# A convolution in 64x64 instead of 32x32 matmul tiles, and all V projections ahead of the spatial mixing

## The chip, the cores and the metric

The kernel runs on all eight cores of one Trainium2 chip (two dies of four cores), one sequence per core. The metric is the device time of the slowest core, in microseconds (us). Most executions agree within 0.3%. Some fall in a second, slower state, in which one die has a lower clock (the kernel before at 2910.64 us: one die's cores at 0.91 to 0.92, the other's at 0.98 to 0.99). The **granted clock** is the TensorE clock that the trace records as allowed, 1.00 being full speed.

Engine names: PE is TensorE (matmuls), PEld its weight loads, ACT is ScalarE, DVE is VectorE, POOL is GpSimd, SP is SyncE, which issues transfers.

## The reference, cut to what matters

One inference step of a decoder trunk with four layers. The part of a layer that matters here:

```python
h = rmsnorm(x, norm1);  z = h @ w_in
# group B: spatial gating inside chunks of 128 rows
b_out = zu * (einsum('hts,bnshc->bnthc', tril(sgu_w), zv) + sgu_b)
# group C: GLU, then a causal depthwise convolution of 31 taps over 384 channels
c_in  = zc[..., :D_C] * sigmoid(zc[..., D_C:])
c_out = silu(layernorm(causal_dwconv(c_in, state, conv_w, conv_b)))
x = x + concat([a_out, b_out, c_out]) @ w_out
x = x + conv_ffn(rmsnorm(x, norm2))
```

Each core has 2048 prompt rows and 64 sample rows. The sample rows need a convolution state that is brought in separately.

## The kernel before

A depthwise convolution has no sum over channels, so on PE it is a banded matrix per channel. The kernel puts 16 channels times 8 time phases on the 128 partitions (a "group"; there are 24). Five shifted matmuls (`k`) cover the 31 taps, and each weight matrix is block diagonal in the channel. Because it is block diagonal it can be cut into small tiles: 4 channels x 8 phases is a 32x32 tile. Two groups (a "pair") are worked on together, `h = 0, 1`. The second one goes to other column strips of the array than the first, so eight of the sixteen 32x32 tiles are in use.

```python
TW = 32
for q in range(12):                                   # twelve pairs
    pb2 = [bank(), bank()]                            # two PSUM banks
    for k in range(NK):                               # 5 shifts
        fin_k = k == NK - 1
        for part in range(1 if fin_k else 2):         # 256 prompt columns, then 16 of the sample state
            for i in range(4):
                for h in range(2):
                    g = 2 * q + h
                    pi = slice(32 * i, 32 * i + 32)
                    po = slice(32 * (i ^ h), 32 * (i ^ h) + 32)
                    src = QS[pi, g, 16*k:16*k+16] if part else Q[j][pi, g % 8, k:k + (MW if fin_k else MB)]
                    dst = pb[po, MB:MW] if part else pb[po, 0:MW if fin_k else MB]
                    matmul(dst, bands.v[j][pi, g % 8, k, :], src, start=(k == 0 and not part), stop=fin_k)
    if q >= 4 and q % 2 == 0: stats(q - 4, q - 2)     # LayerNorm sums, 128x128 matmuls of 272 columns
    # ACT: y[first half] = psum + bias          DVE: y[second half] = psum + bias
    # ACT: sq = square(y)                       POOL: ym = sum of the halves
    # DVE: yq = sum of the halves of sq (of the pair before)
    # [layer 0 only: one step of the pooling of the last tile, on DVE]
```

That is 72 matmuls per pair, each with its own weight load: 144 PE instructions, 1728 per layer. After the convolution the V projections (8 matmuls of 384 columns each), the LayerNorm on DVE, the swishes on ACT and the spatial mixing overlap. V16, V0, V1 come before the convolution, V2 and V3 right after it, then:

```python
for c in range(4, 13):
    vproj(c)
    ...                                   # DVE normalises, ACT applies swish, in between
jobs = [("s", 0), ("v", 13), ("s", 1), ("v", 14), ("v", 15), ("s", 2), ("s", 4), ("s", 3)]
for kind, a in jobs:                      # "s": mixing and gating of tile a, "v": V projection a
    ...
```

The convolution result goes through HBM (a "hop") to return to channel-major order. POOL copies it into place, and the output projection reads it.

Of the kernel before, what the change touches and what calls it, by code (L numbers as in the profile page):

```python
# [11 lines left out]
DEPTH = 4  # L12
# [28 lines left out]
NG = 24  # L41
NK = 5
# [5 lines left out]
SLOT = 2048  # L48
RING = 6 * SLOT
NVB = 17  # L50
TW = 32

class Res:
    __slots__ = ("name", "w", "r", "excl")
# [173 lines left out]
def build_nc():  # L228
# [18 lines left out]
    bnd = din("bnd", [DEPTH, 128, NG * NK * TW])  # L247
# [21 lines left out]
    with ExitStack() as st:  # L269
        S = Sched(nc, st)  # L270
# [22 lines left out]
        AR = Arena(ARENA_T, AW)  # L293
# [31 lines left out]
        DBD = [S.dsem(f"dbd{t}") for t in range(8)]  # L325
# [20 lines left out]
        W = Ring(S, WSA, RING, plan)  # L346

        order = [4, 0, 1, 2, 3]
        order0 = [0, 4, 1, 2, 3]
# [167 lines left out]
        class Bands:  # L517
            def __init__(self, l):
                self.l = l
                self.v, self.R = [], []  # L520
                for b in range(3):
                    v, r = AR.carve(f"dg{b}_", 12768 + 640 * b, 640, 1)
                    self.v.append(v.bitcast(BF16).rearrange("p (g k n) -> p g k n", g=8, k=NK))
                    self.R += r

            def load(self, t):
                S.dma("pool", self.v[t].rearrange("p g k n -> p (g k n)"), bnd[self.l][:, 1280 * t:1280 * (t + 1)], DBD[t], writes=[self.R[t]])

        nrm = Norm(NB, VT_N1)
        nrm.small = AR.carve("sqs", NB, 256, 8)[1]  # L530
# [39 lines left out]
        for l in range(DEPTH):  # L570
            sz_v, Rsz, sc_v, Rsc = stp
            cin, Rcin, Rcs = [], [], []
            for j, a in enumerate((0, 4 * MW, 5308)):
                v, r = AR.carve(f"cin{j}", a, 4 * MW, 2)
# [9 lines left out]
            for j in range(3):  # L584
                S.op("pool", lambda e: e.tensor_copy(cin[j][:, 0:4, MB:MW], sc_v[:, 64 * j:64 * j + 64].rearrange("p (f m) -> p f m", f=4)),
                     reads=[Rsc], writes=[Rcs[j]])
# [278 lines left out]
            vb, Rvb = [None] * NVB, [None] * NVB  # L865

            def vslot_new(c):
                v, r = AR.carve(f"vb{c}_", 14688 + 192 * ((c + 1) % NVB) if c == 16 or c < 13 else 8640 + 192 * (c - 13), 192, 1)
                vb[c], Rvb[c] = v.bitcast(BF16), r[0]

            for i in (16, *range(13)):
                vslot_new(i)
            vs_v, Rvs = AR.carve("vstg", 17376, 384, 1)
            w_v = [W.get(4) for _ in range(2)]
# [1 line left out]
            def vproj(c):  # L876
                rows = 128 if c < 16 else 64
                ti = c // 4
                pb, Rpb = bank()
                for k in range(KC):  # L880
                    S.op("pe", lambda e: e.matmul(pb[0:rows, 0:384], H[:, k, c * 128:c * 128 + rows], w_v[k // 4][1][:, k % 4, :], start=(k == 0), stop=(k == 7)),  # L881
                         reads=[w_v[k // 4][2], RH[k][ti]], writes=[Rpb], inc=(k == 7))
                S.op("act", lambda e: e.copy(vb[c][0:rows], pb[0:rows, 0:384]), reads=[Rpb], writes=[Rvb[c]])  # L883
                if c == 16:
                    S.op("dve", lambda e: e.tensor_copy(vs_v[0:64, 0:384], pb[0:64, 0:384]), reads=[Rpb], writes=[Rvs[0]])
                    out_dma(o_v[l], vs_v[0:64, 0:384], [Rvs[0]], "vstg")
# [6 lines left out]
            for q in range(12):  # L893
                pb2 = [bank(), bank()]
                j = q // 4
                if q % 4 == 0:
                    r0, r1 = [AR.carve(f"y{j}{h}", 2176 * j + 1088 * h, 1088, 4)[1] for h in range(2)]
                    yj.append((ARENA_T[:, 2176 * j:2176 * (j + 1)], r0 + r1))
                rr = [Rq[j][0], Rq[j][1], Rqs, bands.R[j]]
                for k in range(NK):  # L900
                    fin_k = k == NK - 1
                    for part in range(1 if fin_k else 2):
                        for i in range(4):
                            for h in range(2):
                                g = 2 * q + h
                                pi, po = slice(32 * i, 32 * i + 32), slice(32 * (i ^ h), 32 * (i ^ h) + 32)
                                pb, Rpb = pb2[h]
                                src = QS[pi, g, 16 * k:16 * k + 16] if part else Q[j][pi, g % 8, k:k + (MW if fin_k else MB)]
                                dst = pb[po, MB:MW] if part else pb[po, 0:MW if fin_k else MB]
                                S.op("pe", lambda e: e.matmul(dst, bands.v[j][pi, g % 8, k, :], src, start=(k == 0 and not part), stop=fin_k, skip_group_check=True),  # L910
                                     reads=rr, writes=[Rpb], inc=(fin_k and i == 3))
                if q >= 4 and q % 2 == 0:
                    stats(q - 4, q - 2)
                y_v, Ry = yj[j]
                ql = q % 4
                y = y_v[:, ql * 2 * MW:(ql + 1) * 2 * MW]
                cbs = [CVQ[:, 2 * q + h:2 * q + h + 1] for h in range(2)]
                ph = [p_[0][:, 0:MW] for p_ in pb2]
                R0, R1 = pb2[0][1], pb2[1][1]
                Ryq = Ry[2 * ql:2 * ql + 2]  # L920
                sq_v, Rsq_ = sqt[q % 2]
                (ym, Rym), (yq, Ryq2) = sums[2 * (q % 4)], sums[2 * (q % 4) + 1]
                S.op("act", lambda e: e.activation(y[:, 0:MW], ph[0], AF.Identity, bias=cbs[0]), reads=[R0, Rcvq], writes=Ryq[0:1])
                S.op("dve", lambda e: e.tensor_scalar(y[:, MW:2 * MW], ph[1], cbs[1], None, ALU.add), reads=[R1, Rcvq], writes=Ryq[1:2])
                S.op("act", lambda e: e.activation(sq_v, y, AF.Square), reads=Ryq, writes=Rsq_)
                S.op("pool", lambda e: e.tensor_tensor(ym, y[:, 0:MW], y[:, MW:2 * MW], ALU.add), reads=Ryq, writes=Rym)
                while psq:
                    psq.pop(0)()
                psq.append(lambda sq_v=sq_v, Rsq_=Rsq_, yq=yq, Ryq2=Ryq2: S.op("dve", lambda e: e.tensor_tensor(yq, sq_v[:, 0:MW], sq_v[:, MW:2 * MW], ALU.add), reads=Rsq_, writes=Ryq2))
                if steps:  # L930
                    next(steps.pop(0), None)
                if q == 8 and l == 0:
                    assert not steps
                    prep(0)
                    S.dma("sp", FB[:, 0:576], bb_d[0], DM["bb"], writes=[Rfb])
# [1 line left out]
            W.fill()  # L937
            w_u = [W.get(4) for _ in range(2)]
            stats(8, 10)
            for i in (13, 14, 15):  # L940
                vslot_new(i)
            for c in (2, 3):
                vproj(c)
# [109 lines left out]
            def quad():  # L1053
                if quads:
                    j, h = quads.pop(0)
                    ln_quad(j, h)
                    silus.extend((j, h, a) for a in range(4))

            def act_side(n=1):
                for _ in range(n):  # L1060
                    if silus:
                        silu(*silus.pop(0))

            for c in range(4, 13):
                vproj(c)
                if c >= 5:
                    act_side(1)
                if c in (4, 6, 8, 10, 11, 12):
                    quad()
            mixes = [(j, ti) for ti in order0 for j in range(2)]  # L1070
            jobs = [("s", 0), ("v", 13), ("s", 1), ("v", 14), ("v", 15), ("s", 2), ("s", 4), ("s", 3)]
            for kind, a in jobs:
                if kind == "v":
                    vproj(a)
                    if a == 15:
                        for w in w_v:
                            W.done(w[0])
                else:
                    mixed = mixv(a)
                    ts = [addb(a, b, *mixed[b]) for b in range(2)]  # L1080
                    for b in range(3):
                        if b == 1:
                            ts.append(addb(a, 2, *mixed[2]))
                        sgu(a, b, *ts[b])
                        act_side(3 if a == 0 else 2)
                        if mixes and not silus:
                            pmix(*mixes.pop(0))
                    if a in (1, 2, 3):
                        reo[a - 1]()
            while mixes:  # L1090
                pmix(*mixes.pop(0))
            for w in w_u:
# [247 lines left out]

def _conv_rows():
    g, c = np.arange(D_C) // 16, np.arange(D_C) % 16
    return 16 * g + (c ^ (4 * (g % 2)))

def _cat_cols(parts):
    return np.ascontiguousarray(np.concatenate([p.reshape(DEPTH, 128, -1) for p in parts], axis=2))
# [39 lines left out]
    return dict(wt=wt, wts=ws.reshape(DEPTH, 64, 256), bb=np.ascontiguousarray(bb).reshape(DEPTH, 128, 3 * 192))  # L1386

def _phase_layouts(conv_w, conv_b, cnorm_g, cnorm_b):
    bd = np.zeros((DEPTH, 16, 8, NG, NK, 4, 8), np.float32)
    c = np.arange(16)  # L1390
    wg = conv_w.reshape(DEPTH, 31, NG, 16)
    for k in range(NK):
        for fi in range(8):
            for fo in range(8):
                i = 8 * k - 2 + fi - fo
                if 0 <= i < 31:
                    bd[:, c, fi, :, k, c % 4, fo] = wg[:, i].transpose(2, 0, 1)
    vq = np.stack([conv_b, cnorm_g, cnorm_b], axis=1)[:, :, _conv_rows()].reshape(DEPTH * 3 * NG, 16)
    return bd.reshape(DEPTH, 128, NG * NK * TW), np.ascontiguousarray(np.repeat(vq.T, 8, axis=0))

# [69 lines left out]
```

## Time and profile before

| | before |
|---|---|
| kernel time, fast runs | 2731.26 to 2733.41 us |
| PE busy | 97% of the span |
| first convolution matmul to V4, four layers, mean of the cores | 29.5, 31.8, 30.1, 31.1 us |
| V4 to output projection | 45.2, 45.2, 44.7, 44.7 us |

"First convolution matmul to V4" is called **the stage** below. It is read off the trace, core by core, and holds the convolution, V2, V3 and the statistics.

The page of the profile of before (slowest core): its span, PE's share, and PE's busy tenths and granted clock in 40 slices.

```profile
span 2726.5 us, 55276 instructions; the slowest of 8 cores (2716.4 to 2726.5 us)
...
PE 2643.4 (97%) x18494; PEld 1283.8 (47%) x18762; DVE 1724.1 (63%) x2955; ACT 1424.6 (52%) x2705; POOL 600.9 (22%) x840
...
PE   8899999999989999999998999999999899999998
...
PEclk9899999999989999999998999999999999999999
```

The kernel is bound by PE almost everywhere. The few slices below 9 are the places to look at. The windows view of before over the four stages has span, busy time of each engine, granted clock, and DMA share and GB/s:

```profile
93.70:123.90 30.20, 22.09 (x906) 15.00 (x906) 16.36 (x34) 14.60 (x27) 13.72 (x16) 0.72 0.14 36
766.20:799.40 33.20, 23.70 (x905) 15.73 (x905) 8.66 (x24) 14.46 (x26) 11.23 (x16) 0.69 0.20 41
1435.90:1466.40 30.50, 23.44 (x905) 15.35 (x905) 8.78 (x24) 14.54 (x27) 10.69 (x15) 0.72 0.10 26
2102.80:2132.10 29.30, 21.44 (x906) 14.64 (x906) 8.77 (x24) 14.36 (x27) 11.23 (x16) 0.83 0.12 29
```

No engine is near full in any of them (PE 21 to 24 of about 30 us, the others less), and the granted clock is about 0.7. So what is PE waiting for? The timeline of PE in layer 1 (start, length, what; in brackets the idle time before and what ended it; L910 is the convolution, L864 the statistics):

```profile
766.25 1.75 PE L910 MATMUL ps<-arena 32*32 32x256 bf16 x133
768.88 1.77 PE L910 MATMUL ps<-arena 32*32 32x16 bf16 x126 [0.88 <-issue]
773.32 2.05 PE L910 MATMUL ps<-arena 32*32 32x16 bf16 x101 [2.67 <-issue]
...
777.59 2.33 PE L910 MATMUL ps<-arena 32*32 32x256 bf16 x126 [0.63 <-issue]
781.25 1.06 PE L864 MATMUL ps<-arena,oneb 128*128 128x272 bf16 x4 [1.34 <-issue]
```

Two things are to be seen. 126 matmuls take 1.77 us, so PE is fast while it runs. And every gap is ended by "issue": no semaphore and no engine was waited for. The transfer view of before lists the instruction queue; first the 28.5 us of layer 1's convolution, then 28.5 us inside the feed-forward part:

```profile
q8 instruction: 7, 0.11, 1.6%
...
q8 instruction: 1, 0.02, 0.2%
```

The trace records these packets one by one. Here is when each of layer 1 landed (start plus its duration), and when PE issued again after the gap that followed:

```
16,384-byte packet landed at   767.51  771.99  776.25  779.69  784.00  788.28  792.88
PE issues again at             768.88  773.32  777.59  781.25  785.33  789.58  794.31
difference, us                   1.37    1.33    1.34    1.56    1.33    1.30    1.43
```

Every one of the seven packets is followed by a restart of PE 1.3 to 1.6 us later. How many instructions a packet brings can be counted. On all eight cores, the gaps over 0.2 us in layer 1's convolution stand before the same matmuls, the 134th, 260th, 383rd, 509th, 633rd and 758th (statistics counted). They are 123 to 126 matmuls apart, so 246 to 252 instructions with the weight loads. With the semaphore instructions that the trace records for PE there are 255 to 257 instructions from one restart to the next. The whole run agrees: core 1, of which no record is missing, has 40,173 PE instructions and 157 packets, 255.9 per packet.

There are two smaller waits further on: PE waits for DVE in the first mixing tiles (L1026), and in layers 0 and 3 for the reorder copies at the output projection (L1115). The timeline of PE before:

```profile
819.35 0.41 PE L1014 MATMUL ps<-wt_s,arena 128*32 128x128 bf16 x16 [0.35 <-DVE arena L1026]
...
174.29 8.02 PE L1115 MATMUL ps<-arena,wsall 128*128 128x512 bf16 x28 [3.78 <-POOL arena L997]
```

### The profile page before, as it was taken

What the parts mean: (1) busy time and instruction counts of PE and PEld (TensorE: products, weight loads), DVE (VectorE), ACT (ScalarE), POOL (GpSimd) and SP (SyncE); (2) the same over time, 40 slices, a digit from 0 to 9 for tenths busy, and PEclk for the clock granted to TensorE, in tenths of its full rate; (3) what the DMA queues carried; (4) which work ended last, traced back from release to release, by engine and by line L of the source; (5) the groups of instructions that cost most, each with busy time, mean ns of one, the idle gap of its engine ahead of it and who ended that gap; (6) DMA issues with size and microseconds to landing.
All of it is one profiled execution on the core that took longest, in us unless ns stands there. A gap on an engine that the chain in (4) does not pass through costs nothing.

```text
span 2726.5 us, 55276 instructions; the slowest of 8 cores (2716.4 to 2726.5 us)
## 1 busy us (share of the span) xinstructions
PE 2643.4 (97%) x18494; PEld 1283.8 (47%) x18762; DVE 1724.1 (63%) x2955; ACT 1424.6 (52%) x2705; POOL 600.9 (22%) x840
## 2 busy tenths in 40 slices
PE   8899999999989999999998999999999899999998
PEld 3544444444444444444445444444444444444444
DVE  5658656566856765656685675565677567565566
ACT  5446627176354653627535473554753547264575
POOL 4544000003315300000412610000060260000005
PEclk9899999999989999999998999999999999999999
DMA  9342222223233322222223232222223413222213
GB/s 239 87 97 50 37 39 36 39 40 61 50 73 88 56 38 38 37 39 40 53 67 84 60 63 38 38 38 39 40 48 84 108 26 57 40 37 38 40 30 128
DMA packets 82181, 159.56 MB, mean 59 GB/s; under 512 B 10928, under 2 KB 43952, under 8 KB 81840
## 3 DMA queue, kind: packets, MB, share of 16 engines
q0 software_dynamic: 29840, 96.65, 20.9%
q1 hardware_dynamic: 52064, 59.35, 7.1%
q8 instruction: 157, 2.57, 0.4%
q14 instruction: 120, 0.98, 0.1%
HBM read 226.78 MB, written 28.39 MB: 94 GB/s over the span
## 4 chain that ended last, share of the span: by engine, by line
PE 91%; issue 3%; DMA 2%; DVE 2%; ACT 2%; SPq 1%; POOL 0%; DVEq 0%; ACTq 0%; POOLq 0%
PE ps L1205 23%; PE ps L1199 23%; PE ps L1115 16%; PE ps L1277 15%; PE ps L595 7%; PE ps L1037 2%; PE ps L910 2%; PE ps L881 1%; DMA hop<-arena 1%; PE ps L864 1%; DMA X<-win 1%; SPq L139 1%; DMA arena<-hop 0%; DVE H L449 0%; ACT arena L883 0%
## 5 line engine op out<-in xcount | busy, mean ns | idle before, releaser
L1205 PE MATMUL ps<-H,wsall 128*128 128x512 bf16 (+1 forms) x3500 | 697.3, 342 | 1.0
L1199 PE MATMUL ps<-H,wsall 128*128 128x512 bf16 (+1 forms) x3404 | 687.7, 341 | 6.1
L1219 DVE SCALAR_TENSOR_TENSOR arena<-arena,vt_s 128x512 f32<-128x512 f32 (+1 forms) x440 | 289.6, 658 | 384.0 <-ACT arena L1218 367.3
L1214 ACT COPY arena<-ps 128x512 f32<-128x512 f32 (+1 forms) x440 | 223.7, 509 | 575.4 <-PE ps L1199 527.1
L1115 PE MATMUL ps<-arena,wsall 128*128 128x512 bf16 (+2 forms) x2581 | 464.6, 339 | 9.8 <-POOL arena L997 7.3
L1205 PEld LDWEIGHTS ps<-H,wsall 128*128 128x128 bf16 x3520 | 301.8, 98 | 332.6
L1199 PEld LDWEIGHTS ps<-H,wsall 128*128 128x128 bf16 x3520 | 301.8, 98 | 332.6
L1277 PE MATMUL ps<-arena,wsall 128*128 128x512 bf16 (+1 forms) x2200 | 399.1, 342 | 2.1
L1218 ACT ACTIVATE arena<-ps,vt_s 128x512 f32<-128x512 f32 (+1 forms) x440 | 309.0, 702 | 66.0 <-ACT arena L1214 2.8
L1115 PEld LDWEIGHTS ps<-arena,wsall 128*128 128x128 bf16 x2624 | 220.9, 98 | 245.3 <-issue 12.6
L420 POOL TENSOR_TENSOR arena<-arena 128x512 f32<-128x512 f32 (+2 forms) x273 | 293.7, 1076 | 149.2 <-ACT arena L414 119.6
L1221 DVE SCALAR_TENSOR_TENSOR arena<-arena,vt_s 128x512 f32<-128x512 f32 (+1 forms) x440 | 289.5, 658 | 47.0 <-DVE arena L1219 1.4
L1280 DVE TENSOR_TENSOR X<-ps,X 128x512 f32<-128x512 f32 (+1 forms) x320 | 184.5, 595 | 196.5 <-PE ps L1277 196.4
L414 ACT ACTIVATE arena<-X 128x512 f32<-128x512 f32 (+1 forms) x312 | 169.0, 552 | 246.5 <-DVE X L1117 208.0
L1277 PEld LDWEIGHTS ps<-arena,wsall 128*128 128x128 bf16 x2240 | 188.2, 98 | 211.7
L1117 DVE TENSOR_TENSOR X<-ps,X 128x512 f32<-128x512 f32 (+2 forms) x328 | 188.4, 585 | 151.3 <-PE ps L1115 140.1
L1232 DVE TENSOR_TENSOR arena<-arena 128x512 bf16<-128x512 bf16 (+1 forms) x440 | 260.6, 593 | 3.0 <-ACT arena L1231 3.0
L1224 ACT CAST arena<-ps 128x512 bf16<-128x512 f32 (+1 forms) x440 | 223.5, 508 | 59.2 <-PE ps L1205 50.3
L1231 ACT ACTIVATE arena<-arena 128x512 f32<-128x512 f32 (+1 forms) x440 | 245.6, 559 | 15.2 <-DVE arena L1221 15.2
L595 PE MATMUL ps<-H,wsall 128*128 128x512 bf16 (+1 forms) x1252 | 232.1, 343 | 8.9 <-DVE H L449 3.9
L1226 POOL COPY arena<-arena 128x2 f32<-128x2 f32 x88 | 18.0, 205 | 991.0 <-ACT arena L1214 991.0
L449 DVE SCALAR_TENSOR_TENSOR H<-X,vt_s,ps 128x512 bf16<-128x512 f32 (+1 forms) x320 | 207.1, 649 | 27.8 <-ACT ps L438 13.3
(109 smaller groups left out, 1640.1 us busy)
## 6 DMA issues: line engine op xcount, KB each, us to landing
wsall<-wup POOLq DMA_DIRECT2D x88, 512.0 KB, 5.1
wsall<-wdn POOLq DMA_DIRECT2D x32, 448.0 KB, 4.6
hop<-arena SPq DMA_DIRECT2D x24, 544.0 KB, 3.4
arena<-hop SPq DMA_DIRECT2D x24, 544.0 KB, 4.4
X<-xt SPq DMA_DIRECT2D x8, 1024.0 KB, 11.5
wsall<-wout POOLq DMA_DIRECT2D x16, 512.0 KB, 10.3
wsall<-wdn POOLq DMA_DIRECT2D x16, 512.0 KB, 4.9
wsall<-win POOLq DMA_DIRECT2D x16, 384.0 KB, 9.8
```

Of the source, the lines that this page charges most:

```text
L420: S.op("pool", lambda e: e.tensor_tensor(dst, in0, sq, ALU.add), reads=R0 + Rs_, writes=Rd)
L595: S.op("pe", lambda e: e.matmul(pb[:, 0:n], wv[:, k, a:a + 128], H[:, k, c0:c0 + n], start=(k == 0), stop=(k == 7)), reads=[Rw, RH[k][ti]] ...
L1115: S.op("pe", lambda e: e.matmul(pb[:, 0:n], lh, rh, start=(q == 0), stop=(q == len(ops) - 1)), reads=rr, writes=[Rpb], inc=(q == len(ops) ...
L1199: S.op("pe", lambda e: e.matmul(pg[:, 0:n], wv[:, k, 0:128], H[:, k, c0:c0 + n], start=(k == 0), stop=(k == 7)), reads=[Rw, RH[k][ti]], wr ...
L1205: S.op("pe", lambda e: e.matmul(pv[:, 0:n], wv[:, k, 128:256], H[:, k, c0:c0 + n], start=(k == 0), stop=(k == 7)), reads=[Rw, RH[k][ti]], ...
L1214: S.op("act", lambda e: e.copy(G[:, gc:gc + n], pg[:, 0:n]), reads=[Rpg], writes=[gw_])
L1218: S.op("act", lambda e: e.activation(T_, pg[:, 0:n], AF.Identity, bias=fb, scale=w2), reads=[Rpg, Rvt2], writes=[Rtm[q]])
L1219: S.op("dve", lambda e: e.scalar_tensor_tensor(T_, G[:, gc - sh:gc - sh + n], w1, T_, ALU.mult, ALU.add), reads=gr_ + [Rvt2], writes=[Rtm[q]])
L1221: S.op("dve", lambda e: e.scalar_tensor_tensor(T_, G[:, gc - 2 * sh:gc - 2 * sh + n], w0, T_, ALU.mult, ALU.add), reads=gr_ + [Rvt2], writ ...
L1231: S.op("act", lambda e: e.activation(T_, T_, AF.Silu), reads=[Rtm[q]], writes=[Rtm[q]])
L1232: S.op("dve", lambda e: e.tensor_tensor(actb[:, fl, c0:c0 + n], VB_, T_, ALU.mult), reads=[Rvst[q], Rtm[q]], writes=[Rab[fl * 5 + ti]])
L1277: S.op("pe", lambda e: e.matmul(pb[:, 0:n], w[1][:, kk, m2 * 128:(m2 + 1) * 128], actb[:, kk, c0:c0 + n], start=(kk == 0), stop=(kk == nf ...
```

## The change

The intent: use tiles of 8 channels x 8 phases, 64x64, so that four of them fill the whole array and half as many matmuls do the work. The bands (the weight tiles) double in size, which takes the room of most V buffers during the convolution, so V4 to V15 reuse the room that the convolution's input leaves. All V projections are then done before the first mixing tile.

```diff
-TW = 32
+TW = 64
 ...
-                    v, r = AR.carve(f"dg{b}_", 12768 + 640 * b, 640, 1)
+                    v, r = AR.carve(f"dg{b}_", 12768 + 1280 * b, 1280, 1)
 ...
-                        for i in range(4):
-                            for h in range(2):
+                        for h in range(2):
+                            for i in range(2):
                                 g = 2 * q + h
-                                pi, po = slice(32 * i, 32 * i + 32), slice(32 * (i ^ h), 32 * (i ^ h) + 32)
+                                pi, po = slice(64 * i, 64 * i + 64), slice(64 * (i ^ h), 64 * (i ^ h) + 64)
 ...                                                     (V buffers moved, matching weight layout: cut)
-            for c in range(4, 13):
+            for c in range(4, 16):
                 vproj(c)
 ...
-            jobs = [("s", 0), ("v", 13), ("s", 1), ("v", 14), ("v", 15), ("s", 2), ("s", 4), ("s", 3)]
-            for kind, a in jobs:
+            for a in order0:                             # 0, 4, 1, 2, 3: mixing tiles only
 ...
-                        act_side(3 if a == 0 else 2)     # swishes emitted between gatings
+                    act_side(5)
```

More of the change, by code (lines that the diff above doesn't have):

```diff
@@ L526, in load @@
             def load(self, t):
-                S.dma("pool", self.v[t].rearrange("p g k n -> p (g k n)"), bnd[self.l][:, 1280 * t:1280 * (t + 1)], DBD[t], writes=[self.R[t]])
+                S.dma("pool", self.v[t].rearrange("p g k n -> p (g k n)"), bnd[self.l][:, 2560 * t:2560 * (t + 1)], DBD[t], writes=[self.R[t]])
         nrm = Norm(NB, VT_N1)
@@ L867, in vslot_new @@
             def vslot_new(c):
-                v, r = AR.carve(f"vb{c}_", 14688 + 192 * ((c + 1) % NVB) if c == 16 or c < 13 else 8640 + 192 * (c - 13), 192, 1)
+                at = 16608 + 192 * ((c + 1) % NVB) if c in (16, 0, 1, 2) else 14688 if c == 15 else 8640 + 192 * (c - 3)
+                v, r = AR.carve(f"vb{c}_", at, 192, 1)
                 vb[c], Rvb[c] = v.bitcast(BF16), r[0]
-            for i in (16, *range(13)):
+            for i in (16, 0, 1, 2):
                 vslot_new(i)
@@ L910, in build_nc @@
                                 S.op("pe", lambda e: e.matmul(dst, bands.v[j][pi, g % 8, k, :], src, start=(k == 0 and not part), stop=fin_k, skip_group_check=True),
-                                     reads=rr, writes=[Rpb], inc=(fin_k and i == 3))
+                                     reads=rr, writes=[Rpb], inc=(fin_k and i == 1))
                 if q >= 4 and q % 2 == 0:
@@ L939, in build_nc @@
             stats(8, 10)
-            for i in (13, 14, 15):
+            for i in range(3, 16):
                 vslot_new(i)
@@ L1067, in build_nc @@
                     act_side(1)
-                if c in (4, 6, 8, 10, 11, 12):
+                if c in (4, 6, 8, 10, 12, 14):
                     quad()
+            for w in w_v:
+                W.done(w[0])
             mixes = [(j, ti) for ti in order0 for j in range(2)]
-            jobs = [("s", 0), ("v", 13), ("s", 1), ("v", 14), ("v", 15), ("s", 2), ("s", 4), ("s", 3)]
-            for kind, a in jobs:
-                if kind == "v":
-                    vproj(a)
-                    if a == 15:
-                        for w in w_v:
-                            W.done(w[0])
-                else:
-                    mixed = mixv(a)
-                    ts = [addb(a, b, *mixed[b]) for b in range(2)]
-                    for b in range(3):
-                        if b == 1:
-                            ts.append(addb(a, 2, *mixed[2]))
-                        sgu(a, b, *ts[b])
-                        act_side(3 if a == 0 else 2)
-                        if mixes and not silus:
-                            pmix(*mixes.pop(0))
-                    if a in (1, 2, 3):
-                        reo[a - 1]()
+            for a in order0:
+                mixed = mixv(a)
+                ts = [addb(a, b, *mixed[b]) for b in range(2)]
+                for b in range(3):
+                    if b == 1:
+                        ts.append(addb(a, 2, *mixed[2]))
+                    sgu(a, b, *ts[b])
+                    act_side(5)
+                    if mixes and not silus:
+                        pmix(*mixes.pop(0))
+                if a in (1, 2, 3):
+                    reo[a - 1]()
             while mixes:
@@ L1342, in _conv_rows @@
     g, c = np.arange(D_C) // 16, np.arange(D_C) % 16
-    return 16 * g + (c ^ (4 * (g % 2)))
+    return 16 * g + (c ^ (8 * (g % 2)))
 def _cat_cols(parts):
@@ L1388, in _phase_layouts @@
 def _phase_layouts(conv_w, conv_b, cnorm_g, cnorm_b):
-    bd = np.zeros((DEPTH, 16, 8, NG, NK, 4, 8), np.float32)
+    bd = np.zeros((DEPTH, 16, 8, NG, NK, 8, 8), np.float32)
     c = np.arange(16)
@@ L1396, in _phase_layouts @@
                 if 0 <= i < 31:
-                    bd[:, c, fi, :, k, c % 4, fo] = wg[:, i].transpose(2, 0, 1)
+                    bd[:, c, fi, :, k, c % 8, fo] = wg[:, i].transpose(2, 0, 1)
     vq = np.stack([conv_b, cnorm_g, cnorm_b], axis=1)[:, :, _conv_rows()].reshape(DEPTH * 3 * NG, 16)
```

## The prediction

> **What bounds the kernel now.** The profile has TensorE busy 97% of 2726.5 us; the chain of waits is 91% PE. It starves in one stage per layer, the convolution (L910). In the timeline, from its first matmul to V projection 4 (L881) takes 30.2, 33.2, 30.5 and 29.3 us in the four layers: 123 us. The windows view has the granted clock there at 0.69 to 0.83.
>
> The records show eight 32x32 tiles starting about 4 ns apart, and a step (eight of 256 columns, eight of 16) taking 0.15 us, so a pair of groups (72 matmuls) needs about 0.75 us. The stage spends about 2.3 us per pair, with PE gaps of 1.5 to 3.9 us released by "issue", no semaphore. In layer 1's convolution (28.5 us) the instruction queue moves seven 16 KB packets, one every 3.5 to 4.5 us; elsewhere about one per 20 us. [...] 12 pairs x 144 instructions are 6.75 blocks; x 3.9 us = 26 us. So PE instruction fetch bounds the stage[...].
>
> **What the change does.** 64x64 tiles halve the instructions (864 to 432 matmuls per layer, weight loads likewise), at the same streamed columns per step: four tiles fill the array where eight used half. The convolution needs about 3.5 blocks[...]. Next in line are ACT (bias 0.49 plus square 0.66 us, overlapped about 1.05 us per pair) and PE (0.75 plus 0.28 for the statistics). With V2, V3 (2.6 us) and the last statistics I expect 17 to 19 us from first convolution matmul to V4: 11 to 14 us less per layer, about 50 in all.
>
> V first: DVE's twelve normalisation steps (1.29 us each) finish about 19 us after V4 begins. Today PE waits for them (L1026), idle 2.6 us per layer. With twelve V's (15.8 us) ahead, 1.5 us of it goes: 6 us. The swishes end earlier, so the hop through HBM returns before the output projection; layers 0 and 3 stall 3.8 and 3.5 us on POOL L997 there: about 6 us.
>
> Cost: band transfers double (320 to 640 KB each); at the start, where DMA is saturated (300 GB/s), a tile may land 1 to 2 us late.
>
> **Sum:** 50 + 6 + 6 - 2 = 60 us. Predicted 2671 us, range 2652 to 2700. Chances: faster by over 2% 0.64, within 2% 0.35, slower 0.01.
>
> **What would show it.** Right: instruction packets per convolution fall to 3 or 4; "issue" gaps over 1 us vanish; the stage to V4 is 17 to 19 us with the clock above 0.85; from V4 to the output projection 43 us in place of 45, without the POOL L997 wait. Wrong: gaps stay with half the packets, or the stage stays above 22 us.
>
> **What would make it wrong.** (1) The clock: at half clock a pair takes 1.3 us plus 0.5 of statistics, and the stage about 25 us. (2) 64x64 tiles sharing rows do not overlap as 32x32 ones do, or their weight loads (64 columns) do not hide. (3) ACT, DVE and PE handing banks to each other pace the pairs at 1.4 us rather than 1.1. (4) V's no longer fill PE's waits between mixing tiles.

The "blocks" are the packets of 16,384 bytes, 256 PE instructions each by the count above, so 1728 instructions are 6.75. The "half clock" is a granted clock of 0.50, as in layer 1 of before at 777.59 us, where 126 matmuls take 2.33 us, 1.33 per pair; four statistics take 1.09 us at that clock (at 109.13 us), 0.54 per pair. "Saturated" is a DMA share of 0.97 to 1.01 at 295 to 302 GB/s from 30 to 50 us of before.

## The result, and the profile after

| | before | after |
|---|---|---|
| kernel time, median | 2732.68 us | 2670.74 us |
| fast runs | 2731.26 to 2733.41 | 2669.19 to 2674.02 |
| ratio | | 0.9777 (95% interval 0.9757 to 0.9796) |

The median of before takes in one slow run (2864.72 us); the median of its fast runs is 2731.95 us. A ratio is the mean time of one kernel's fast runs over that of the other's fast runs of the same rounds, so it is not quite the ratio of the medians.

The page after, the lines that answer to those of before:

```profile
span 2673.0 us, 52102 instructions; the slowest of 8 cores (2664.2 to 2673.0 us)
...
PE 2636.3 (99%) x17034; PEld 1274.9 (48%) x17034; DVE 1726.8 (65%) x2955; ACT 1420.9 (53%) x2705; POOL 601.1 (22%) x840
...
PE   8999999999999999999999999999999999999998
...
PEclk9999999999999999999999999999999999999999
```

PE is busy for nearly the same time (2636 against 2643 us) in a span 53 us shorter: the time came out of PE's idle. The windows view after, over the four stages (slowest core):

```profile
94.90:119.50 24.60, 20.11 (x474) 13.69 (x474) 17.48 (x34) 13.89 (x27) 13.19 (x16) 0.86 0.21 48
755.20:772.60 17.40, 15.74 (x473) 12.10 (x473) 8.99 (x24) 13.57 (x27) 10.72 (x16) 1.00 0.16 44
1408.00:1428.70 20.70, 18.54 (x473) 13.64 (x473) 9.05 (x24) 13.97 (x27) 9.18 (x12) 0.84 0.14 36
2064.10:2084.00 19.90, 15.64 (x473) 12.01 (x473) 8.96 (x24) 13.88 (x27) 10.94 (x16) 1.00 0.17 40
```

The stages are 5.6 to 15.8 us shorter on the slowest cores, with 473 matmuls instead of 905. The timeline of PE in layer 1, and the instruction queue in its convolution (14.2 us):

```profile
755.24 3.92 PE L911 MATMUL ps<-arena 64*64 64x256 bf16 x176
759.70 0.31 PE L911 MATMUL ps<-arena 64*64 64x272 bf16 x4 [0.54 <-issue]
759.94 0.64 PE L864 MATMUL ps<-arena,oneb 128*128 128x272 bf16 x4
760.51 1.55 PE L911 MATMUL ps<-arena 64*64 64x256 bf16 x72
...
764.06 0.99 PE L911 MATMUL ps<-arena 64*64 64x256 bf16 x35 [0.52 <-issue]
```

```profile
q8 instruction: 3, 0.05, 1.4%
```

Two pairs (72 matmuls) now take 1.55 us, and the gaps are half a microsecond. The two later waits, timeline of PE after: the gap in the mixing is 0.80 us, and the output projection of layer 0 starts and runs without a wait:

```profile
796.73 0.39 PE L1038 MATMUL ps<-H,wsall 128*128 128x64 bf16 x8 [0.80 <-ACT arena L1047]
...
163.36 9.01 PE L1111 MATMUL ps<-arena,wsall 128*128 128x512 bf16 x41
```

Where the time came from, as means over the eight cores of the two profiles, all four layers added:

| part | before | after | difference |
|---|---|---|---|
| mean span of a core | 2721.9 | 2667.3 | -54.6 us |
| start to first convolution matmul, layer 0 | 93.4 | 94.4 | +1.0 |
| the four stages | 122.4 | 77.2 | -45.2 |
| V4 to output projection | 179.7 | 175.6 | -4.1 |
| PE idle at the start of the output projection | 5.0 | 0.3 | -4.6 |
| rest, not itemised | | | -1.7 |

The kernel time fell by more (61 us by the fast runs), since it counts the slowest core and since the profiled run of before was a little faster than its timed ones: in the timed fast runs of before whose cores are listed (the rounds of the first four experiments) the mean core takes 2723.8 to 2724.9 us and the slowest 2728.0 to 2731.4.

### The profile page after: what moved, and what is told of

Same layout as the page of the kernel before. It is cut to its first block, busy times and chain, and to the rows that moved or that the text cites. A ratio compares the mean times of both kernels' runs of the same rounds, so it can differ in the third digit from the quotient of the medians.

```text
span 2673.0 us, 52102 instructions; the slowest of 8 cores (2664.2 to 2673.0 us)
## 1 busy us (share of the span) xinstructions
PE 2636.3 (99%) x17034; PEld 1274.9 (48%) x17034; DVE 1726.8 (65%) x2955; ACT 1420.9 (53%) x2705; POOL 601.1 (22%) x840
## 4 chain that ended last, share of the span: by engine, by line
PE 95%; DVE 1%; issue 1%; ACT 1%; SPq 1%; DMA 1%; POOL 0%; DVEq 0%; ACTq 0%; POOLq 0%
PE ps L1195 24%; PE ps L1201 24%; PE ps L1111 17%; PE ps L1273 15%; PE ps L595 7%; PE ps L882 3%; PE ps L1038 3%; PE ps L911 1%; SPq L139 1%; DMA X<-win 1%; PE ps L1015 1%; PE ps L864 0%; DVE H L449 0%; PE ps L426 0%; DVE arena L649 0%
## 5 line engine op out<-in xcount | busy, mean ns | idle before, releaser
L1195 PE MATMUL ps<-H,wsall 128*128 128x512 bf16 (+1 forms) x3520 | 700.2, 342 | 0.0
L1201 PE MATMUL ps<-H,wsall 128*128 128x512 bf16 (+1 forms) x3520 | 700.2, 342 | 0.0
L1222 POOL COPY arena<-arena 128x2 f32<-128x2 f32 x88 | 18.1, 206 | 991.8 <-ACT arena L1210 991.8
L595 PE MATMUL ps<-H,wsall 128*128 128x512 bf16 (+1 forms) x1280 | 234.1, 343 | 6.5 <-DVE H L449 3.9
L449 DVE SCALAR_TENSOR_TENSOR H<-X,vt_s,ps 128x512 bf16<-128x512 f32 (+1 forms) x320 | 207.2, 650 | 28.9 <-ACT ps L438 14.1
```

The costliest lines, as they stand in the source:

```text
L595: S.op("pe", lambda e: e.matmul(pb[:, 0:n], wv[:, k, a:a + 128], H[:, k, c0:c0 + n], start=(k == 0), stop=(k == 7)), reads=[Rw, RH[k][ti]] ...
L1195: S.op("pe", lambda e: e.matmul(pg[:, 0:n], wv[:, k, 0:128], H[:, k, c0:c0 + n], start=(k == 0), stop=(k == 7)), reads=[Rw, RH[k][ti]], wr ...
L1201: S.op("pe", lambda e: e.matmul(pv[:, 0:n], wv[:, k, 128:256], H[:, k, c0:c0 + n], start=(k == 0), stop=(k == 7)), reads=[Rw, RH[k][ti]], ...
```

## The experiments

My theory: the stage was bound by the supply of PE instructions, and halving their number is what gained. Rivals: the 32x32 tiles themselves are slow, as they leave half the array unused; or the new order carries the gain. Eleven kernels were run; the result is right unless said otherwise. The ratio is to the kernel before on the same chip. Stage times are means over the eight cores.

### The two halves of the change, one at a time

`conv_only`: the changed kernel, with the job list of before put back.

```diff
-            for c in range(4, 16):
+            for c in range(4, 13):
 ...
-            for a in order0:
+            jobs = [("s", 0), ("v", 13), ("s", 1), ("v", 14), ("v", 15), ("s", 2), ("s", 4), ("s", 3)]
```

> The 64x64 tiles alone, with the old order of V projections and mixing tiles. My theory (instruction fetch bounded the convolution): the stage from first convolution matmul to V4 falls from 29-34 us per layer to 17-25 us as in the full change, 3 or 4 instruction packets per stage; from V4 to the output projection stays at 44.7-45.0 us and the 3.5-3.8 us waits on the reorder copies (POOL) at the output projection in layers 0 and 3 stay. Total about 2682 us (saves 47 to 53). Rival (most of the gain is the new order, the tiles only shift idle time): saves under 25 us.

Measured: ratio 0.9835 (0.9818 to 0.9851), median 2686.05 us. It saved about 45 us, a little less than the 47 to 53 I expected. Stages 23.2, 17.4, 18.1, 18.8 us, as in the full change; V4 to output projection 44.8 to 45.2 us, as before. The wait at the output projection is still there, though on this run's slowest core in layer 1 (timeline of PE):

```profile
826.38 5.95 PE L1116 MATMUL ps<-arena,wsall 128*128 128x512 bf16 x19 [3.26 <-POOL arena L998]
```

`order_only`: the kernel before (32x32 tiles) with the new job list; the diff is the reverse one.

> The new order alone (all V projections before the first mixing tile), with 32x32 tiles. My theory: convolution stage unchanged (29-34 us per layer, 7 packets, granted clock about 0.7), V4 to output projection falls from about 44.8 to 43.9 us, the reorder waits at the output projection in layers 0 and 3 go; saves 8 to 12 us, total about 2722 us. Rival (the order carries the gain): saves over 30 us.

Measured: ratio 0.9963 (0.9945 to 0.9981), median 2721.13 us over all its runs, fast ones 2717.86 to 2722.73. Stages 30.4, 31.0, 30.3, 31.3 us (7 or 8 packets each, clock 0.71 to 0.76): unchanged. V4 to output projection 43.9 to 44.0 us, and the idle at the output projection gone (0.3 us for the four layers).

The two ratios multiply to 0.980, and the whole change measured 0.978. Within the intervals that is the same: about 45 us from the tiles, about 10 us from the order, 61 us together. The 6 us between the sum and the whole are within the uncertainty.

### Few instructions in 32x32 tiles, many in 64x64 tiles

`few32`: the kernel before without the 16-column matmuls for the sample state; each step streams 272 columns instead of 256 and 16, so the same columns in 40 matmuls per pair instead of 72. The sample rows are wrong.

```diff
-                    for part in range(1 if fin_k else 2):
+                    for part in range(1):
 ...
-                                src = ... Q[j][pi, g % 8, k:k + (MW if fin_k else MB)]
-                                dst = ... pb[po, 0:MW if fin_k else MB]
+                                src = ... Q[j][pi, g % 8, k:k + MW]
+                                dst = ... pb[po, 0:MW]
```

> Kernel before, still 32x32 tiles, but the separate 16-column matmuls for the sample state are left out and every step streams 272 columns instead: the same columns through the array, 40 matmuls per pair instead of 72. Wrong result on purpose: the sample rows' convolution is wrong, the prompt's is not. Fetch theory: 80 instructions per pair, nearly the 72 of the changed kernel, so the stage falls to 18-23 us per layer, 4 packets, issue gaps over 1 us mostly gone; total about 2685 us (saves 40 to 50). Rival (half-filled array, 32x32 tiles themselves slow): stage stays at 28 us or more, total 2715 or more.

Measured: ratio 0.9855 (0.9831 to 0.9878), fast runs 2687.11 to 2697.79 us (three of its six runs were slow). Stages 23.1, 19.0, 19.9, 19.4 us, 4 to 5 packets. The windows view of its layer 1, and the instruction queue in that convolution (14.1 us):

```profile
759.10:778.40 19.30, 15.32 (x522) 10.03 (x522) 9.08 (x24) 13.72 (x26) 11.26 (x16) 1.00 0.17 42
...
q8 instruction: 4, 0.07, 1.9%
```

So 32x32 tiles in half the array are nearly as fast as 64x64 tiles in all of it, once there are as few instructions (mean stage 20.3 us with 80 instructions per pair, against 19.3 with 72).

`split4`: the changed kernel with every prompt matmul cut into four, the columns unchanged: 192 instructions per pair.

```diff
+                                ns = 1 if part else 4
+                                for s_ in range(ns):
+                                    a_, w_ = s_ * wd_ // ns, wd_ // ns     # wd_: 256, 272 or 16 columns
-                                src = ... Q[j][pi, g % 8, k:k + (MW if fin_k else MB)]
+                                    src = ... Q[j][pi, g % 8, k + a_:k + a_ + w_]
```

> Changed kernel (64x64 tiles, new order) with each 256- or 272-column convolution matmul cut into four of 64 or 68 columns: the same columns, 96 matmuls per pair instead of 36, so 192 instructions instead of 72. Result stays right. Fetch theory: 2300 convolution instructions per layer are 9 blocks; [...] at 3.9 us each, the stage is 31-37 us per layer, with 9 or 10 packets and gaps, and the granted clock falls below 0.85; total 2720 to 2740 us (50 to 70 over the changed kernel). Rival (array filling, not fetch): stage 18-23 us, total 2670 to 2685.

Measured: ratio 1.0057 (1.0039 to 1.0075), median 2746.38 us: slower than the kernel before, with the tiles of the fast one. Stages 40.0, 38.8, 37.6, 37.0 us, 9 or 10 packets, clock 0.65 to 0.70. The windows view of layer 1, then the timeline of PE, which shows the gaps of before again:

```profile
771.50:811.50 40.00, 26.04 (x1193) 20.51 (x1193) 8.59 (x24) 14.78 (x27) 11.22 (x16) 0.70 0.11 24
...
771.50 1.25 PE L916 MATMUL ps<-arena 64*64 64x64 bf16 x102
773.33 1.74 PE L916 MATMUL ps<-arena 64*64 64x64 bf16 x126 [0.58 <-issue]
777.75 1.71 PE L916 MATMUL ps<-arena 64*64 64x16 bf16 x127 [2.69 <-issue]
781.40 2.19 PE L916 MATMUL ps<-arena 64*64 64x64 bf16 x125 [1.95 <-issue]
```

The stage was longer than I expected (31 to 37 us), and so was the time. The packet rate alone accounts for it. Over all cores and layers packets land 3.95 us apart on average, exactly as in before, and the convolution takes 34.3 us on average for its 2304 instructions, nine packets of 256; nine times 3.95 us are 35.6. The passage cut above took two packets off, an estimate that no run shows: hardly one was saved. V2, V3 and the last statistics add 4.1 us.

`split2`: the same with a cut in two, 112 instructions per pair.

> Changed kernel with each 256- or 272-column convolution matmul cut in two: 56 matmuls per pair, 112 instructions; the same columns; result right. Fetch theory, worked out from the run with 192 instructions (mean stage 38.4 us): 960 instructions fewer are 3.75 packets of 3.9 us, so 23-25 us per layer on average, 5 or 6 packets, total 2685 to 2697 us. A theory in which each cut costs array time only (short matmuls) gives a third of what the cut in four cost: mean stage 25-26 us and 4 packets; a theory with a threshold far above 112 gives 19-20 us.

Measured: ratio 0.9859 (0.9845 to 0.9873), median 2689.15 us, stages 23.6, 23.9, 23.0, 24.8 us (mean 23.8), 5 to 6 packets. PE idle per stage 5.5 to 6.7 us.

`few64`: the changed kernel without the 16-column matmuls (the edit of `few32`), 40 instructions per pair. Its output is wrong, which doesn't matter for the time.

> Changed kernel without the separate 16-column state matmuls (272 columns at every step): 20 matmuls, 40 instructions per pair. Wrong result on purpose (sample rows). If ScalarE now paces the convolution (1.18 us per pair in the trace), fetch no longer matters: stages of layers 1 to 3 stay within 0.7 us of the changed kernel's 17.7, 18.0 and 18.5 us, total 2665 to 2671 us, with the remaining PE gaps explained by waits for PSUM banks. If instruction supply still limits, stages fall by 2 us or more each, total below 2662 us.

Measured: ratio 0.9776 (0.9762 to 0.9790), median 2666.99 us. Stages 22.8, 16.9, 17.2, 17.0 us, so 0.7, 0.9 and 1.5 us below the changed kernel in layers 1 to 3. That is more than I expected if nothing but ScalarE paced, and less than if supply still bound: in the changed kernel late instructions still cost about a microsecond per layer. The gaps over 0.2 us that are left in the changed kernel's layers 1 to 3 are again 121 or 122 matmuls apart, 255 to 257 PE instructions with weight loads and semaphore instructions, one packet. No control ran on the chip of this run, so its ratio shows no gain in time over the changed kernel.

Put together, in the order of instructions per pair:

| instructions per pair | 40 | 72 | 80 | 112 | 144 | 192 |
|---|---|---|---|---|---|---|
| tiles | 64x64 | 64x64 | 32x32 | 64x64 | 32x32 | 64x64 |
| run | few64 | after | few32 | split2 | before | split4 |
| mean stage, us | 18.5 | 19.3 | 20.3 | 23.8 | 30.6 | 38.4 |

The columns streamed through each row strip of the array (the rows that one tile takes) are the same in all six. The stage follows the number of instructions, whatever the tile, down to a floor at about 18.5 us.

### What sets the floor

`l0_nosteps`: layer 0 stayed at 23.0 us. In the changed kernel's trace DVE does pooling steps there (L649, among others) between the evictions (L925) and sums (L930) that free the banks and feed the statistics. The timeline of DVE, layer 0, after:

```profile
97.61 0.45 DVE L930 TENSOR_TENSOR arena<-arena 128x272 bf16<-128x272 bf16 x1
97.98 1.34 DVE L649 SCALAR_TENSOR_TENSOR arena<-fb,cstt 128x512 f32<-128x512 f32 x1
99.25 0.49 DVE L925 TENSOR_SCALAR arena<-ps,cvq_s 128x272 f32<-128x272 f32 x1
```

An eviction that takes 0.49 us waits for 1.34 us of pooling. The run leaves out the shifted adds of that tile (wrong):

```diff
                 src, Rsrc = z, [Rzz]
+                if l == 0 and ti == 3:
+                    sh_list = []
```

> Changed kernel; in layer 0 the shifted adds of the last pooling tile, which VectorE does between convolution evictions, are left out (2 VectorE operations stay of 8). Wrong result on purpose. If these are why layer 0's stage is 23.0 us and not 18 as in the other layers: it falls to 18-20 us, other layers unchanged, total 3 to 5 us less. If the start (data landing late, clock) is the reason: it stays above 22 us.

Measured: layer 0's stage 18.6 us instead of 23.0, with the clock at 1.00 there instead of 0.94; the others 19.2, 17.8, 18.7. The ratio (0.9778, 0.9761 to 0.9794) cannot tell it from the changed kernel, as no control ran on this chip. The cause of the longer stage is shown; a gain in time is not. Of the 4.4 us, 2.5 lie in the convolution itself (16.4 against 13.9 us, at clock 1.00 on every core in both). The rest lies in V2, V3 and the last statistics, where five of the eight cores of the changed kernel had a clock of 0.58 to 0.75.

`act_relief`: in layer 1 after, ACT goes through the pairs without a pause. The timeline of ACT, after (L924 bias, L926 square):

```profile
758.87 0.47 ACT L924 ACTIVATE arena<-ps,cvq_s 128x272 f32<-128x272 f32 x1
759.49 0.66 ACT L926 ACTIVATE arena<-arena 128x544 bf16<-128x544 f32 x1
760.05 0.47 ACT L924 ACTIVATE arena<-ps,cvq_s 128x272 f32<-128x272 f32 x1
```

A pair every 1.18 us, twelve of them 14.2 us. The run gives every second first-half bias to DVE.

```diff
+                if l and q % 2:
+                    S.op("dve", lambda e: e.tensor_scalar(y[:, 0:MW], ph[0], cbs[0], None, ALU.add), ...)
+                else:
                     S.op("act", lambda e: e.activation(y[:, 0:MW], ph[0], AF.Identity, bias=cbs[0]), ...)
```

> Changed kernel; in layers 1 to 3, in every second pair, the bias add of the first half moves from ScalarE to VectorE. If ScalarE paces the convolution at 1.18 us per pair: its load falls to about 0.95 us per pair, PE (0.78 + 0.28 us) becomes the limit, stages of layers 1 to 3 fall by 0.7 to 1.7 us each, total 2 to 5 us less than the changed kernel. If PE or instruction supply paces: no change (within 1 us), or slower because the bank is freed later by VectorE.

Measured: ratio 0.9789 (0.9775 to 0.9803), no faster than the changed kernel's. Stages 22.7, 17.3, 17.1, 18.5: down 0.4 and 1.0 us in layers 1 and 2, nothing in layer 3. ACT now waits for DVE instead:

```profile
760.22 0.66 ACT L929 ACTIVATE arena<-arena 128x544 bf16<-128x544 f32 x1 [0.26 <-DVE arena L928]
761.76 0.66 ACT L929 ACTIVATE arena<-arena 128x544 bf16<-128x544 f32 x1 [0.88 <-DVE arena L928]
```

So ScalarE's pace is one of several limits that lie close together; taking it away alone gains nothing that shows in the time.

### A faster version

PE still idles 1.6 to 4.7 us in each stage of the changed kernel. The three V projections ahead of the convolution (4.1 us of PE work in few instructions) can fill that. `spread`:

```diff
-            for c in (16, 0, 1):
-                vproj(c)
 ...
+                if q in (2, 5, 8):                # after pairs 2, 5 and 8 of the convolution
+                    vproj({2: 16, 5: 0, 8: 1}[q])
```

The windows view of `spread` in layer 1, V's included:

```profile
744.20:765.60 21.40, 20.28 (x494) 14.04 (x493) 11.70 (x29) 14.81 (x29) 9.65 (x13) 1.00 0.21 63
```

`after_again`, the control, is the changed kernel unedited. `spread_relief` is `spread` with the edit of `act_relief`.

> The changed kernel once more, as control on the chip of the next two runs: 0.976 to 0.979 of the kernel before, stages 23, 17.7, 18.0, 18.5 us within 1 us.

> Changed kernel; the three V projections that stood ahead of the convolution (V16, V0, V1, 4.1 us) are put between its pairs (after pairs 2, 5 and 8). Theory: PE's remaining idle in the convolution (2 to 5 us per layer: instruction supply a little late, ScalarE and VectorE pacing) is filled by them, since they need few instructions and no eviction of a pair. From the convolution's first matmul to V4 (V's included) 20 to 21.5 us in layers 1 to 3 against 4.1 + 17.7 to 18.5 before, about 24 in layer 0 against 27; total 4 to 8 us less than the control. Rival (ScalarE is full, its three more copies of 0.48 us lengthen the stage): no gain or slower.

> The same with every second pair's first bias add moved from ScalarE to VectorE in layers 1 to 3. If ScalarE paces the spread stage: another 2 to 4 us less than spread. If PE does: within 1 us of spread.

| same chip, five rounds | ratio to before | fast runs, us | stages, us |
|---|---|---|---|
| after_again | 0.9782 (0.9768 to 0.9796) | 2668.95 to 2672.26 | 23.0, 17.6, 17.6, 18.5, after 4.1 of V each |
| spread | 0.9753 (0.9739 to 0.9767) | 2661.46 to 2664.66 | 23.2, 21.4, 20.3, 20.9, V's included |
| spread_relief | 0.9778 (0.9748 to 0.9808) | 2664.95 to 2666.76, one 2689.01 | 23.5, 22.2, 20.7, 21.1, V's included |

`spread` beats both kernels: 8.9 us less than the control by the medians of the fast runs (2662.56 against 2671.50), a little more than the 4 to 8 I expected, and every one of its fast runs is below every one of the control's. With V's its stages take 85.8 us in the four layers, against 76.6 + 4 x 4.1 = 93.0. PE's idle in the stage falls to 0.5 to 1.1 us in layers 1 to 3 and 2.6 us in layer 0, and the clock there is 1.00 in all layers. The relief on top of it makes it slower, which I did not expect and which speaks against ScalarE as the one limit. Its ratio takes in the 2689.01 us run, in which one die had a clock of 0.986 against 0.998; but its other fast runs, too, all lie above those of `spread`.

## Why the prediction was right

The predicted time (2671 us) is the measured one (2670.74 us). The mechanism was right; that the number was hit this closely is luck, as the terms are not all exact.

- *Fetch bounds the stage.* Right, and shown both ways: `few32` is fast and `split4` slow against their tile sizes. The packets fell to 3 or 4 as forecast. In the convolutions of before a packet landed every 3.9 us (median over all cores and layers; 3.1 to 5.2), and PE issued again 1.0 to 1.65 us after one. Until its first gap over 0.5 us PE ran 266 to 472 instructions of a layer's convolution, so one to two packets' worth came without a wait.
- *50 us from the stages.* They gave 45.2. Layers 1 to 3 came to 17.7, 18.0 and 18.5 us, inside 17 to 19. Layer 0 came to 23.0, above the 22 that the prediction had named as a sign of being wrong, because DVE carries pooling there (`l0_nosteps`: 18.6), which the prediction did not count.
- *"Issue" gaps over 1 us vanish.* Not quite. The eight cores of the profile still show 17 gaps of 1.1 to 2.1 us in layers 1 to 3. `few64` puts what supply still costs at about 1 us per layer.
- *ACT at about 1.05 us per pair is next in line.* It was 1.18, and relieving it did not pay; ACT then waited for DVE, so these engines seem to lie close together there.
- *6 us from the order in the mixing, 6 us from the hop.* 4.1 and 4.6 us. `order_only` gave both without the tiles. From V4 to the output projection it is 43.9 us, not 43.
- *2 us lost at the start.* Not shown. The convolution of layer 0 starts 1.0 us later in the profile and 0.4 us later in the control, but these starts scatter: 94.2 us in `order_only` with the small bands, 93.2 in `split2` with the large ones.
- *The clock in the stage is above 0.85.* Right on the mean of the cores; what lowers it was not shown. Low clocks and long idle mostly go together: the stage's clock was 0.72 to 0.77 with 7.4 to 9.0 us of PE idle per stage (before), 0.65 to 0.70 with 11.5 to 13.1 (`split4`), 0.94 to 0.99 with 1.6 to 4.7 (after). But `split2` has 5.5 to 6.7 us of idle and 0.92 to 0.99, and `few32` 3.5 to 5.4 and 0.89 to 0.97. What the low clock cost can be read from the cores of one run, which had the same instructions at different clocks. In layer 0 of before the convolution, first to last matmul, takes 26.2 us both on the core at 0.61 and on the one at 0.87. Over its 32 convolutions (eight cores, four layers), each compared with its layer's mean, a clock higher by 0.1 goes with 0.2 us less time (correlation -0.1, so no trend) and 1.3 us more idle: a faster core only waited longer for instructions. V2, V3 and the last statistics after it take 4.6 us on average and 3.5 at best, at clock 1.00, so there a low clock can cost about 1 us per layer at most. So nearly all of the 45 us is supply, by this comparison of cores; no run set the clock. Where supply does not bind, the clock counts: in layer 2 of after one core at 0.80 takes 17.2 us for the convolution, the others at 1.00 take 13.5 to 14.6.

The sum was closer than its terms: they came out 5 us short in the stages, 3 us short in the rest and 1 us better at the start, and the slowest core gained more than the mean core did.

Two more things are measured. ACT runs without a pause at 1.18 us per pair in layer 1 of after, but only 0.47 us of this empties PSUM, and ACT was not the only limit. And the matmuls of the two row tiles of a group, which write to different partitions of one PSUM bank, start 3 or 4 ns apart in after in 80% of the cases, take 166 ns or more each in the trace, and the result is right.

## What to carry to other kernels

When PE idles, and the profile names no semaphore for it ("issue"), count its instructions against the packets of the instruction queue: here 256 instructions arrived per 3.9 us, and small tiles with many short matmuls outran that. Then cut the number of instructions (larger tiles, wider matmuls), or mix the dense stretch with work that needs few instructions, as the spread V projections do. After the fix several engines lay close together here (relieving ACT of its 1.18 us per pair gained nothing in the time), so test a supposed next limit before building on it.
